# Shift and scale in couples, tokens in pairs of tiles, sums by transposes, Toeplitz products in column groups

## The chip, the cores and the metric

The kernel runs on one core of one Trainium2 chip. The metric is the device time of one execution in microseconds (us), as a median over runs.

## The reference, cut to what matters

One layer of a diffusion backbone: 1024 latent tokens and 256 context tokens of width 1024. The first two of six modulation vectors (a shift and a scale, from `c` for the latent tokens and from `c_ctx` for the context) act on the normalised tokens; one projection `w_in` follows. Its first 256 columns feed a bidirectional S5 (state space) block, the rest six gated heads over chunks of 128 tokens. After an output projection come a residual, a layer norm and a mixture of 16 experts.

```python
mod_lat = (silu(c) @ w_ada + b_ada)          # 6 vectors of 1024: sh1, sc1, g1, sh2, sc2, g2
mod_ctx = (silu(c_ctx) @ w_ada + b_ada)
z  = (layer_norm(x)   * (1 + sc1)  + sh1)  @ w_in
zc = (layer_norm(ctx) * (1 + csc1) + csh1) @ w_in[:, :256]
mix = concat(s5(z[:, :256], zc), heads(gelu(z[:, 256:]))) @ w_out
x_new = layer_norm(ALPHA * x + g1 * mix)
out = layer_norm(ALPHA * x_new + g2 * expert_choice_moe(modulate(x_new, sh2, sc2)))
```

In float32; large products are made as three products of a high and a low part (`wh`, `wl`, `xmH`, `xmL`).

## The kernel before

Every engine works its own queue in the order in which the program was written out; there is no scheduler. Ten token tiles of 128 rows are `items` 0 and 1 (context) and 2 to 9 (latent). For each, `tok_stats` and `tok_norm` normalise the rows on VectorE with two small GpSimd steps for the root, `tok_turn` transposes the tile on TensorE in two halves, `tok_mod` scales and shifts it on ScalarE (eight 128-wide activations and two copies that give `xmH`) and takes `xmL` on VectorE. Then `z_s5` projects the tile onto the S5 columns (24 products) and stores the result, and `unit` runs one head on one latent tile: 24 products in `head_a`, activation, statistics, and a small product in `head_p` three units later.

Shift and scale come from eight pieces of `w_ada` of 1 MB each, 256 outputs a piece. `ada_piece` multiplies one in four column groups of 32 (16 passes on TensorE, since a float32 product takes two); `ada_cols` then sums the four groups and turns the result into columns by a product with `combo`. All eight pieces are worked before anything is modulated; `mod1` is finished in two VectorE operations, and the loop over tiles starts. The S5 block runs as two generators, `lift_flow` and `s5_flow`; `pull` advances them between tile steps. Its set-up (`params`) works with many small operations on VectorE, and one part, `turns`, on GpSimd. `toeplitz` makes, four times, a small matrix from 8 products with 32 weights each, adds the diagonal and sends it through DRAM. `ada_b` turns later pieces into the second shift and scale. `conv_w` splits a weight block into `wh` (ScalarE) and `wl` (VectorE; for the S5 columns a quarter on GpSimd). Transposes write to two PSUM banks (`trp`), products to two (`mm`).

TensorE's queue does the pieces, waits for what it needs, and goes on to heads, output projection, router, and 528 blocks of expert weights. SyncE issues the loads in the order of `START`; a load waits for an earlier one or for its buffer.

Of the kernel before, what the change touches and what calls it, by code (L numbers as in the profile page):

```python
# [10 lines left out]
F32 = mybir.dt.float32  # L11
# [17 lines left out]
PULL0 = 9  # L29
# [21 lines left out]
MDVE = ()  # L51
START = "a0 a1 a2 a3 a4 a5 x0 a6 a7 w0 x1 x2 p w1".split()
PULLA = 2
# [9 lines left out]
PULLS = 2  # L63
W8 = 6
W9 = 8
N1 = 0
XB = 3
# [6 lines left out]
class S5:  # L74
# [7 lines left out]
    def __init__(self, nc, pool, psum, psum_tr, ident, id2, dcol):  # L82
        self.nc, self.ps, self.ptr = nc, psum, psum_tr
        self.ident, self.id2, self.dcol = ident, id2, dcol
        self.half = [pool, pool]
# [60 lines left out]

    def load_c(self, src):
        self.pc = self.t("pc", 2, 256).rearrange("p a b -> p (a b)")
        self.nc.sync.dma_start(self.pc, src[:, 560:1072])

    def params(self):
# [37 lines left out]
        self.turns(nc.gpsimd, cs, parts(1344, 4, 8), pw2, sq2, w[:, 22:24])  # L189
# [30 lines left out]
        yield  # L220

# [11 lines left out]

        t4, pw = parts(384, 4, 8), parts(896, 2, 10)
# [6 lines left out]
    def turns(self, v, cs, t, pw, sq, ph):  # L241
# [4 lines left out]
        self.cmul(b, a, a, t1, v)  # L246
        c = [x[:, :, 1:2] for x in pw]
        self.cmul(c, b, b, t1, v)
        self.cmul(b, c, c, t1, v)

# [7 lines left out]
        steps = self.powers(pw, b, 16, t, sq, v)  # L258
        while True:
            try:  # L260
                next(steps)
            except StopIteration as e:
                w8 = e.value
                break
# [64 lines left out]
    def toeplitz(self, q, dma, tz):  # L329
        nc, v = self.nc, self.nc.vector  # L330
        t0 = self.t("t0", 2, 16, 16)[0:32]
        ps = self.ptr()
        for d in range(2):
            for r in range(2):
                cc = d * 2 + r
                for i in range(2):
                    nc.tensor.matmul(ps[0:32, cc * 128:(cc + 1) * 128], self.bz[i][:, cc, :],
                                     self.cx[i][:, cc, d:d + 8, :].rearrange("p b h -> p (b h)"),
                                     start=(i == 0), stop=(i == 1))
        x = ps.rearrange("p (d r b h) -> p d r b h", d=2, r=2, b=8)[0:32]  # L340
        nc.scalar.activation(t0[:, :, 7:15, :], x[:, 0], AF.Copy)
        nc.scalar.activation(t0[:, :, 0:7, :], x[:, 1, :, 0:7], AF.Copy)
        nc.scalar.activation(t0[:, :, 15, :], x[:, 1, :, 7], AF.Copy)
        yield "pause"
        v.tensor_tensor(t0[:, :, 7], t0[:, :, 7], t0[:, :, 15], OP.add)
        for r in range(2):
            v.scalar_tensor_tensor(t0[:, r, 7, :], self.id2[0:32], self.dcol[0:32, 2 * q + r:2 * q + r + 1],
                                   t0[:, r, 7, :], op0=OP.mult, op1=OP.add)
        yield "pause"
        dma(tz[q], t0.rearrange("p r b h -> p (r b h)"))  # L350
# [83 lines left out]
def block_kernel(ctx: ExitStack, tc: tile.TileContext, a: dict, out: bass.AP):  # L434
# [35 lines left out]
    src = [a["w_ada"][i] for i in range(8)] + [a["w_in"][i] for i in range(3)]  # L470
# [119 lines left out]
    s5 = S5(nc, A_, acp2, trp, ident, off["id2"], off["dcol"])  # L590
    s5.load(a["s5par"])

# [26 lines left out]
    def tok_turn(i):  # L619

        if i >= NI:
            return
        xt = tok.pop(i)[0]
        turned[i] = []
        for half in range(2):
            p = trp()
            for c in range(4):
                k = 4 * half + c
                pe.transpose(p[:, c * 128:(c + 1) * 128], xt[:, k * 128:(k + 1) * 128], ident)
            turned[i].append(p)  # L630

    def take(i):

        kind, t = items[i]
        s = slice(t % 2 * 128, t % 2 * 128 + 128)
        return [x[:, :, s] for x in xm[kind, t // 2]]

    def tok_mod(i, parts=(0, 1)):

        if i >= NI:  # L640
            return
        kind, t = items[i]
        if t % 2 == 0 and 0 in parts:
            xm[kind, t // 2] = [slot(n, "big", [128, 8, 256], F32R) for n in ("xmH", "xmL")]
        mod = mod1[:, :, 0 if kind == "x" else 1]
        hi, lo = take(i)
        for half in parts:
            p = turned[i][half]
            t = X_.tile([128, 4, 128], F32, name="xmt", bufs=2)
            for c in range(4):  # L650
                k = 4 * half + c
                x = p[:, c * 128:(c + 1) * 128]
                if (i, half) in MDVE:
                    v.tensor_scalar(t[:, c], x, mod[:, 8 + k:9 + k], mod[:, k:k + 1], op0=OP.mult, op1=OP.add)
                else:
                    act.activation(t[:, c], x, AF.Identity, scale=mod[:, 8 + k:9 + k], bias=mod[:, k:k + 1])
            s = slice(4 * half, 4 * half + 4)
            act.activation(hi[:, s], t, AF.Copy)
            v.tensor_tensor(lo[:, s], t, hi[:, s].bitcast(F32), OP.subtract)

    def ada_piece(i, p):

        t = raw.pop(i).rearrange("p (k n) -> p k n", k=8)
        for r in range(2):
            for c in range(4):
                k = 2 * c + r
                pe.matmul(p[32 * c:32 * c + 32], s_t[:, k, :], t[:, k, :], start=(r == 0), stop=(r == 1),
                          tile_position=(0, 32 * c))

# [27 lines left out]
    def z_s5(i):  # L697
# [4 lines left out]
        p = mm()  # L702
        proj(p[:, 0:256], *take(i), ws5)
        z = X_.tile([128, 256], F32, name="zs5", bufs=2)
        act.activation(z, p[:, 0:256], AF.Copy)
# [152 lines left out]
    pull(PULL0)  # L858
    tok_stats(0)
    tok_norm(0)  # L860
    pull(PULLA)
    cols1 = acp2()
    ws = W_.tile([128, 6, 128], F32, name="ws")

    def ada_cols(i, rows):
        for c in range(2):
            k = 2 * i + c
            pe.matmul(cols1[:, 2 * k:2 * k + 2], rows[:, c * 128:(c + 1) * 128], combo[:, 0:2], start=True, stop=True)

    rows = []  # L870
    for i in range(8):
        p = mm()
        ada_piece(i, p[:, 0:256])
        rows.append(X_.tile([128, 256], F32, name="arow", tag="xmt", bufs=2))
        act.activation(rows[i], p[:, 0:256], AF.Copy)
        if i:
            ada_cols(i - 1, rows[i - 1])
    ada_cols(7, rows[7])
    tok_turn(0)
    c1 = cols1[:, 0:32].rearrange("p (c o) -> p c o", o=2)  # L880
    v.tensor_tensor(mod1, c1, bc(bcol[:, 0:16], [128, 16, 2]), OP.add)
    v.tensor_scalar(mod1[:, 8:16], mod1[:, 8:16], 1.0, None, op0=OP.add)
    tok_load(3)
# [87 lines left out]
    def ada_b(n):  # L971
# [8 lines left out]
        for c in range(4):  # L980
# [883 lines left out]
```

## Time and profile before

| | |
|---|---|
| median of 3 runs | 2026.65 us (2026.36 to 2029.82) |
| the profiled execution: time, span | 2030.29 us, 2028.5 us |
| mean granted TensorE clock | 0.994 |
| TensorE busy | 1971.9 us, 97% of the span |
| VectorE, ScalarE, GpSimd busy | 84%, 65%, 14% |
| bytes read from memory | 620.79 MB |

Times in the rows below are microseconds from the start of the span. A row in brackets names idle time of the engine just ahead of the instruction and what ended it. Matmul rows overlap, so the distance of two starts says more than a length.

### The profile page before, as it was taken

The numbers are of one execution on the slowest core, as the hardware profiler recorded it, in microseconds if no ns is written. First come the engines' busy times: TensorE is split into PE (matmuls) and PEld (weight loads), VectorE is DVE, ScalarE is ACT, GpSimd is POOL, SyncE is SP. The second block draws the span as 40 slices with busy tenths as digits, with TensorE's granted clock in tenths as the row PEclk, the third lists the DMA queues.
The fourth block names the chain that finished last, engine by engine and source line by source line (L and its number), as shares of the span: only waits on it lengthen the run. The fifth ranks groups of instructions, "written<-read, shape, count | busy, mean of one in ns | idle before, by whom it ended". The sixth has DMA issues, their size and how long they took to land. (4 is left out here: it accounts for less than half of the span.)

```text
span 2028.5 us, 27963 instructions
## 1 busy us (share of the span) xinstructions
PE 1971.9 (97%) x10690; PEld 1601.8 (79%) x10690; DVE 1709.7 (84%) x1770; ACT 1325.6 (65%) x1497; POOL 287.8 (14%) x462
## 2 busy tenths in 40 slices
PE   6999999989999999999999999999999999999997
PEld 4988897856788787888888888888788888888874
DVE  7678756978798988888898989898989888888876
ACT  3854453224677677767777777767777777677773
POOL 4343353120010101010000101010101010100024
PEclk9999999999999999999999999999999999999999
DMA  8244336379999999999999999999999999999795
GB/s 320 83 151 143 103 115 230 117 281 364 335 388 362 383 362 387 363 377 366 378 359 387 363 380 367 378 373 367 375 371 378 361 384 358 391 362 362 283 385 193
DMA packets 105434, 648.32 MB, mean 320 GB/s; under 512 B 11794, under 2 KB 19986, under 8 KB 33236
## 3 DMA queue, kind: packets, MB, share of 16 engines
q1 hardware_dynamic: 88788, 614.00, 79.0%
q0 software_dynamic: 6080, 23.87, 4.3%
q10 hardware_dynamic: 10432, 8.66, 1.3%
q8 instruction: 84, 1.38, 0.3%
q14 instruction: 50, 0.41, 0.1%
HBM read 620.79 MB, written 24.40 MB: 318 GB/s over the span
## 5 line engine op out<-in xcount | busy, mean ns | idle before, releaser
L1629 DVE TENSOR_TENSOR el<-raw,eh 128x2048 fp32r<-128x2048 f32 x513 | 1174.6, 2290 | 169.1 <-ACT eh L1628 147.7
L1628 ACT ACTIVATE eh<-raw 128x2048 fp32r<-128x2048 f32 x513 | 963.5, 1913 | 67.0 <-PE ac L1724 46.1
L1696 PE MATMUL mm<-eh,XH 128*128 128x512 f32 (+1 forms) x1484 | 566.3, 382 | 0.0
L1697 PE MATMUL mm<-el,XH 128*128 128x512 f32 (+1 forms) x1484 | 557.4, 376 | 0.0
L1698 PE MATMUL mm<-eh,XL 128*128 128x512 f32 (+1 forms) x1484 | 557.2, 375 | 0.0
L1697 PEld LDWEIGHTS mm<-el,XH 128*128 128x128 f32 x1484 | 279.6, 188 | 54.4 <-DVE el L1629 2.9
L1698 PEld LDWEIGHTS mm<-eh,XL 128*128 128x128 f32 x1484 | 279.6, 188 | 53.2
L1696 PEld LDWEIGHTS mm<-eh,XH 128*128 128x128 f32 x1484 | 279.5, 188 | 52.0 <-ACT raw L1562 1.2
L1722 PE MATMUL ac<-eh,tH 128*128 128x512 f32 x692 | 276.0, 399 | 0.0
L1724 PE MATMUL ac<-eh,tL 128*128 128x512 f32 x692 | 272.8, 394 | 0.0
L1723 PE MATMUL ac<-el,tH 128*128 128x512 f32 x692 | 272.2, 393 | 0.4 <-DVE el L1629 0.4
L1734 POOL DMA_INDIRECT acc_d<-yt,idx x15 | 50.7, 3381 | 1156.5 <-DVE yt L1732 1156.5
L1701 ACT ACTIVATE hs<-mm 128x512 f32<-128x512 f32 x96 | 54.1, 563 | 205.2 <-PE mm L1698 201.8
L1724 PEld LDWEIGHTS ac<-eh,tL 128*128 128x128 f32 x692 | 129.9, 188 | 30.3
L1723 PEld LDWEIGHTS ac<-el,tH 128*128 128x128 f32 x692 | 129.9, 188 | 29.7 <-DVE el L1629 0.8
L1722 PEld LDWEIGHTS ac<-eh,tH 128*128 128x128 f32 x692 | 130.0, 188 | 28.5 <-issue 0.5
L691 PE MATMUL mm<-wh,xmH 128*128 128x256 f32 x464 | 136.7, 295 | 5.7 <-ACT uv L905 5.7
L692 PE MATMUL mm<-wl,xmH 128*128 128x256 f32 x464 | 132.3, 285 | 2.5 <-DVE wl L686 2.5
L693 PE MATMUL mm<-wh,xmL 128*128 128x256 f32 x464 | 132.2, 285 | 0.0
L1648 ACT ACTIVATE tH<-tr 128x512 fp32r<-128x512 f32 x94 | 52.9, 562 | 92.7 <-PE tr L1640 91.7
L691 PEld LDWEIGHTS mm<-wh,xmH 128*128 128x128 f32 x464 | 89.8, 193 | 10.6 <-ACT uv L905 7.8
L1210 ACT ACTIVATE xgt<-tr,mod 128x128 f32<-128x128 f32 x124 | 55.5, 454 | 59.7 <-PE tr L1523 59.6
(416 smaller groups left out, 2092.4 us busy)
## 6 DMA issues: line engine op xcount, KB each, us to landing
raw<-in_w_moe SPq DMA_DIRECT2D x523, 1024.0 KB
raw<-in_w_ada SPq DMA_DIRECT2D x24, 1024.0 KB
raw<-in_w_in SPq DMA_DIRECT2D x7, 1024.0 KB
raw<-in_w_moe POOLq DMA_DIRECT2D x5, 1024.0 KB, 10.3
xt<-in_x SPq DMA_DIRECT2D x8, 512.0 KB
raw<-in_w_out SPq DMA_DIRECT2D x4, 1024.0 KB
xr<-in_x SPq DMA_DIRECT2D x8, 512.0 KB
acc_d<-accst ACTq DMA_DIRECT2D x8, 512.0 KB
```

The lines of the kernel that those rows point to most:

```text
L691: pe.matmul(p, xh[:, k], w[0][:, k], start=(k == 0), stop=False)
L692: pe.matmul(p, xh[:, k], w[1][:, k], start=False, stop=False)
L693: pe.matmul(p, xl[:, k], w[0][:, k], start=False, stop=(k == 7))
L1210: act.activation(out, p, AF.Identity, scale=mod2[:, 8 + k:9 + k], bias=mod2[:, k:k + 1])
L1628: act.activation(h, x, AF.Copy)
L1629: v.tensor_tensor(l, x, h.bitcast(F32), OP.subtract)
L1696: pe.matmul(p, XH[:, k], hh[:, c], start=(k == 0), stop=False)
L1697: pe.matmul(p, XH[:, k], ll[:, c], start=False, stop=False)
L1698: pe.matmul(p, XL[:, k], hh[:, c], start=False, stop=(k == 7))
L1722: pe.matmul(y, tH[:, sl], hh[:, c, m], start=first, stop=False)
L1723: pe.matmul(y, tH[:, sl], ll[:, c, m], start=False, stop=False)
L1724: pe.matmul(y, tL[:, sl], hh[:, c, m], start=False, stop=last)
```

## The change

The eight pieces are now worked in couples: a piece of the shift and the piece of the scale for the same 256 columns (0 and 4, 1 and 5, 2 and 6, 3 and 7). Each piece's row is copied to SBUF, turned by two transposes (`ada_turns`), and VectorE sums the four groups out of PSUM and adds the bias (`ada_mod`). After each couple a quarter of the channels can be modulated, and `z_part` adds this quarter to the S5 projection of both context tiles. Tokens go in pairs of tiles: `pair_turn` and `pair_mod` work a quarter of the channels of two tiles at a time, with scalings of 256 columns. `turns` becomes a generator that `side` advances between the other steps. The token loads are spread between the pieces. In the loop, pair g+1 is transposed and modulated while pair g is projected. `toeplitz` puts its products side by side in four column groups and adds the diagonal in one operation from a prepared tile; its result is stored by two transfers for one. `ada_b` sums by transposes too.

```diff
-START = "a0 a1 a2 a3 a4 a5 x0 a6 a7 w0 x1 x2 p w1".split()
+START = "x0 a0 a4 x1 a1 a5 w0 x2 a2 a6 x3 a3 a7".split()
-XB = 3
+XB = 4
...
-        self.turns(nc.gpsimd, cs, parts(1344, 4, 8), pw2, sq2, w[:, 22:24])
+        self.side = self.turns(nc.gpsimd, cs, parts(1344, 4, 8), pw2, sq2, w[:, 22:24])
...
     def toeplitz(self, q, dma, tz):
-        t0 = self.t("t0", 2, 16, 16)[0:32]
+        t0 = self.t("t0", 8, 16)
         ps = self.ptr()
-        for d in range(2):
+        for i in range(2):
+            for half in range(2):
+                for r in range(2):
+                    cc = (1 - half) * 2 + r
+                    o = 64 * half + 32 * r
+                    nc.tensor.matmul(ps[o:o + 32, 0:128], self.bz[i][:, cc, :],
+                                     self.cx[i][:, cc, 1:9, :].rearrange("p b h -> p (b h)"),
+                                     start=(i == 0), stop=(half == 1 and i == 1), tile_position=(0, o))
+        for i in range(2):
             for r in range(2):
-                cc = d * 2 + r
-                for i in range(2):
-                    nc.tensor.matmul(ps[0:32, cc * 128:(cc + 1) * 128], self.bz[i][:, cc, :],
-                                     self.cx[i][:, cc, d:d + 8, :].rearrange("p b h -> p (b h)"),
-                                     start=(i == 0), stop=(i == 1))
+                nc.tensor.matmul(ps[32 * r:32 * r + 32, 112:128], self.bz[i][:, r, :], self.cx[i][:, r, 0, :],
+                                 start=False, stop=(i == 1), tile_position=(0, 32 * r))
...
-    def tok_turn(i):
...
+    def pair_turn(g, j, p, tiles=(0, 1)):
+        for n in tiles:
+            for c in range(2):
+                k = 2 * j + c
+                pe.transpose(p[:, 256 * c + 128 * n:256 * c + 128 * n + 128],
+                             tok[2 * g + n][0][:, k * 128:(k + 1) * 128], ident)
+        turned[g, j] = p
...
-    def tok_mod(i, parts=(0, 1)):
...
+    def pair_mod(g, j):
...
+        for c in range(2):
+            k = 2 * j + c
+            act.activation(t[:, c], p[:, 256 * c:256 * c + 256], AF.Identity, scale=mod[:, 8 + k:9 + k],
+                           bias=mod[:, k:k + 1])
+        s = slice(2 * j, 2 * j + 2)
+        hi, lo = xm[g]
+        act.activation(hi[:, s], t, AF.Copy)
+        v.tensor_tensor(lo[:, s], t, hi[:, s].bitcast(F32), OP.subtract)
...
+    def ada_turns(j, s, rows):
+        if s == 0:
+            at_c[j] = acp()
+        for c in range(2):
+            o = 256 * s + 128 * c
+            pe.transpose(at_c[j][:, o:o + 128], rows[:, c * 128:(c + 1) * 128], ident)
+
+    def ada_mod(j):
+        c = W_.tile([128, 4, 2], F32, name="c1", bufs=2)
+        x = at_c[j].rearrange("p (m g r) -> p m r g", g=4, r=32)[:, :, 0:2]
+        v.tensor_reduce(c, x, axis=mybir.AxisListType.X, op=OP.add)
...
+    pair_mod(0, 1)
     ws5 = conv_w(8, W8)
...
+    rows = [ada_rows(4)]
+    tok_norm(2)
+    ada_turns(2, 0, rows[0])
+    z_part(0)
+    z_part(1)
+    rows.append(ada_rows(5))
+    ada_turns(2, 1, rows[1])
+    ada_mod(2)
+    pair_mod(0, 2)
+    tok_stats(3)
+    side(2)
+    pull(1)
+    tok_norm(3)
+    z_part(2)
...
-        for c in range(4):
-            pe.matmul(p[:, 2 * c:2 * c + 2], rows[:, c * 128:(c + 1) * 128], combo[:, 0:2], start=True, stop=True)
         j = 4 * (n - 2)
+        ada_turn(p, rows, m, 1)
...
-    for i in range(NI):
...
+    for g in range(1, NI // 2):
+        last = g == NI // 2 - 1
...
+        ahead = (0, 1, 2, 3) if g > 1 else (None, 0, 1, 2)
+        for j in range(4):
+            pairwise = g > 1 and not last
+            n = j // 2 if pairwise else j % 2
+            if not last and ahead[j] is not None:
+                pair_turn(g + 1, ahead[j], trp())
+            if j in ((0, 2) if pairwise else (0, 1)):
+                z_s5(2 * g + n)
+            else:
+                unit(2 * g - 2 + n)
+            if not last and ahead[j] is not None:
+                pair_mod(g + 1, ahead[j])
...
+            if j in (0, 2):
+                tok_stats(2 * g + 4 + j // 2)
+            else:
+                tok_norm(2 * g + 4 + j // 2)
+            pull(PULL1 if g > 1 or j == 3 else 0)
```

On ScalarE, in the ramp: `arow` is the copy of a piece's row out of PSUM, `xmt` a scaling, `xmH` the high part, `wh` the high part of the S5 weights. Before:

```order
L875 ACTIVATE arow<-mm 128x256 [waits PE_49] x2
L875 ACTIVATE arow<-mm 128x256 [waits PE_49,Activation_49] x6
L683 ACTIVATE wh<-raw 128x2048 [waits DMAHW5_49]
L656 ACTIVATE xmt<-tr,mod_125 128x128 [waits DVE_49,PE_49,Activation_49]
L656 ACTIVATE xmt<-tr,mod_125 128x128 x3
L658 ACTIVATE xmH<-xmt 128x4x128 [waits DMAHW4_49,Activation_49]
```

and in the change, from the fourth piece's copy on:

```order
L876 ACTIVATE arow<-mm 128x256 [waits PE_49]
L652 ACTIVATE xmt<-tr,mod_126 128x256 [waits DVE_49]
L652 ACTIVATE xmt<-tr,mod_126 128x256
L656 ACTIVATE xmH<-xmt 128x512 [waits Activation_49]
L689 ACTIVATE wh<-raw 128x2048 [waits DMAHW4_49]
L876 ACTIVATE arow<-mm 128x256 [waits PE_49] x2
```

All eight row copies stood ahead of the weights; now the weights stand between the fourth copy and the last four, behind two couples of scalings.

On TensorE, `tr<-sp,xt` are token transposes and the other rows products. Before, the transposes of item 5 behind the second head unit:

```order
L692 MATMUL mm<-wl,xmH 128x256
L693 MATMUL mm<-wh,xmL 128x256
L629 MATMUL tr<-sp,xt 128x128 [waits DVE_49,Activation_49]
L629 MATMUL tr<-sp,xt 128x128 x3
L629 MATMUL tr<-sp,xt 128x128 [waits Activation_49]
L629 MATMUL tr<-sp,xt 128x128 x3
L691 MATMUL mm<-wh,xmH 128x256 [waits Activation_49]
L692 MATMUL mm<-wl,xmH 128x256
```

and in the change, at the end of the loop's first trip, behind the second head unit:

```order
L698 MATMUL mm<-wl,xmH 128x256
L699 MATMUL mm<-wh,xmL 128x256
L634 MATMUL tr<-sp,xt 128x128 [waits PE_49,Activation_49]
L634 MATMUL tr<-sp,xt 128x128 x3
L634 MATMUL tr<-sp,xt 128x128 [waits DVE_49,PE_49,Activation_49]
L634 MATMUL tr<-sp,xt 128x128
L634 MATMUL tr<-sp,xt 128x128 [waits DVE_49]
L634 MATMUL tr<-sp,xt 128x128
```

Here the transposes of two pairs follow each other; the second group needs both tiles of the next pair normalised, its last two rows the second of them.

On VectorE at the same place, `xt<-xt,mv,rstd` is a normalisation and `xmL` the low part of a modulated tile. Before, the normalisation of item 4 with its statistics ahead:

```order
L582 BN_STATS st<-xt 128x6 [waits DMAHW5_49]
L582 BN_STATS st<-xt 128x6
L562 BN_AGGR mv<-st 128x2 [waits DVE_49]
L617 TENSOR_SCALAR xt<-xt,mv,rstd 128x1024 [waits DVE_49,PE_49,Pool_49]
L659 TENSOR_TENSOR xmL<-xmt,xmH 128x4x128 [waits Activation_49] x2
```

and in the change the second normalisation of that next pair:

```order
L657 TENSOR_TENSOR xmL<-xmt,xmH 128x512 [waits Activation_49]
L591 BN_STATS st<-xt 128x6 [waits DMAHW3_49]
L591 BN_STATS st<-xt 128x6
L571 BN_AGGR mv<-st 128x2 [waits DVE_49]
L657 TENSOR_TENSOR xmL<-xmt,xmH 128x512 [waits Activation_49]
L627 TENSOR_SCALAR xt<-xt,mv,rstd 128x1024 [waits DVE_49,PE_49,Pool_49]
```

The normalisation stood right behind its statistics and ahead of the subtractions of item 3; now a subtraction of the pair in work stands between a tile's statistics and its normalisation.

## Rows read from the trace of the kernel before

**Rows 1.** Windows view, stretches in us; busy time per engine (instructions), clock, DMA share, GB/s

```profile
10.00:20.00 10.00, 9.54 (x73) 4.41 (x74) 8.94 (x54) 1.47 (x5) 6.96 (x32) 1.00 1.01 423
...
315.00:320.00 5.00, 4.47 (x11) 3.27 (x12) 4.49 (x5) 3.04 (x8) 3.92 (x4) 0.66 0.42 150
...
600.00:1000.00 400.00, 399.35 (x1906) 326.70 (x1905) 355.98 (x224) 294.98 (x228) 23.73 (x8) 1.00 0.98 373
```

**Rows 2.** Timeline of TensorE, 9 to 65 us; start, length, line, operation, idle before

```profile
9.94 1.94 PE L667 MATMUL mm<-raw,s_t 128*32 128x256 f32 x16 [9.94 <-DMA raw<-in_w_ada]
...
39.95 1.94 PE L629 MATMUL tr<-sp,xt 128*128 128x128 f32 x8 [4.82 <-DVE xt L617]
...
41.90 0.41 PE L692 MATMUL mm<-wl,xmH 128*128 128x256 f32 x1
...
42.12 0.41 PE L693 MATMUL mm<-wh,xmL 128*128 128x256 f32 x1
...
50.25 0.36 PE L691 MATMUL mm<-wh,xmH 128*128 128x256 f32 x1
...
53.20 0.28 PE L691 MATMUL mm<-wh,xmH 128*128 128x256 f32 x1
...
54.57 0.39 PE L692 MATMUL mm<-wl,xmH 128*128 128x256 f32 x1 [1.09 <-DVE wl L686]
...
64.57 1.03 PE L629 MATMUL tr<-sp,xt 128*128 128x128 f32 x8
```

**Rows 3.** Timeline of ScalarE, 31 to 73 us

```profile
31.93 1.90 ACT L683 ACTIVATE wh<-raw 128x2048 fp32r<-128x2048 f32 x1
...
34.36 1.50 ACT L656 ACTIVATE xmt<-tr,mod 128x128 f32<-128x128 f32 x4 [0.53 <-PE tr L629]
...
36.43 1.49 ACT L656 ACTIVATE xmt<-tr,mod 128x128 f32<-128x128 f32 x4
...
71.39 0.28 ACT L904 ACTIVATE uv<-mm 128x128 f32<-128x128 f32 x1 [1.33 <-PE mm L693]
...
72.20 0.48 ACT L930 ACTIVATE uv<-uv,hst 128x128 f32<-128x128 f32 x1
```

**Rows 4.** Timeline of VectorE, 13 to 44 us

```profile
13.82 0.17 DVE L201 TENSOR_TENSOR scr<-scr,par 128x16 f32<-128x16 f32 x1
...
15.26 0.46 DVE L215 TENSOR_TENSOR bbr<-scr,par 128x256 f32<-128x256 f32 x1
...
17.98 0.11 DVE L223 TENSOR_TENSOR scr<-scr 128x16 f32<-128x16 f32 x1
...
35.28 1.71 DVE L686 TENSOR_TENSOR wl<-raw,wh 128x1536 fp32r<-128x1536 f32 x1
...
42.84 0.81 DVE L617 TENSOR_SCALAR xt<-xt,mv,rstd 128x1024 f32<-128x1024 f32 x1 [1.00 <-POOL rstd L564]
...
43.56 0.68 DVE L659 TENSOR_TENSOR xmL<-xmt,xmH 128x512 fp32r<-128x512 f32 x1
```

**Rows 5.** Timeline of GpSimd, 35 to 42 us

```profile
35.46 1.61 POOL L563 TENSOR_SCALAR rstd<-mv 128x1 f32<-128x1 f32 x1 [5.09 <-DVE mv L562]
...
41.93 0.22 POOL L563 TENSOR_SCALAR rstd<-mv 128x1 f32<-128x1 f32 x1 [2.68 <-DVE mv L562]
```

**Rows 6.** Timeline of TensorE, 109 to 316 us

```profile
109.16 0.39 PE L692 MATMUL mm<-wl,xmH 128*128 128x256 f32 x1 [1.38 <-DVE wl L686]
...
112.32 1.07 PE L667 MATMUL mm<-raw,s_t 128*32 128x256 f32 x16
...
119.79 0.41 PE L337 MATMUL tr<-cx,bzr 128*32 128x128 f32 x2 [0.25 <-ACT U L768]
...
121.66 0.38 PE L691 MATMUL mm<-wh,xmH 128*128 128x256 f32 x1
...
315.53 0.50 PE L1040 MATMUL mm<-woH,mh 128*128 128x512 f32 x1 [3.73 <-ACT mh L1026]
```

**Rows 7.** Waits of TensorE, 100 to 350 us: total, times, longest

```profile
PE mm L691 <- ACT uv L905: 5.7, 6, 1.7
```

More of the change, by code (lines that the diff above doesn't have):

```diff
@@ L28 @@
 PPE = 33
-PULL0 = 9
 PULL1 = 1
@@ L62 @@
 TLEAD = 2
-PULLS = 2
 W8 = 6
 W9 = 8
-N1 = 0
-XB = 3
+XB = 4
 def bc(ap, shape):
@@ L232, in params @@
         yield
+        for _ in self.side:
+            pass
         t4, pw = parts(384, 4, 8), parts(896, 2, 10)
@@ L257, in turns @@
             v.tensor_tensor(b[c], b[c], x, OP.mult)
[L258 to L264, printed above, removed]
+        yield
+        w8 = yield from self.powers(pw, b, 16, t, sq, v)
         self.cmul([x[:, :, 3:4] for x in sq], w8, w8, t1, v)
@@ L857, in block_kernel @@
     mod2 = K.tile([128, 16], F32, name="mod2")
[L858 to L862, printed above, removed]
-    ws = W_.tile([128, 6, 128], F32, name="ws")
[L865 to L871, printed above, removed]
+    bias1 = W_.tile([128, 2, 8], F32, name="bias1")
+    pool.tensor_copy(bias1, bcol[:, 0:16].rearrange("p (s k) o -> p s (k o)", s=2))
@@ new lines, in block_kernel, with z_part @@
+    zp = bank("rk")
+    zps = [zp[:, 256 * n:256 * n + 256] for n in range(2)]
+    def z_part(j):
+        for n in range(2):
+            proj(zps[n], *take(n), ws5, (2 * j, 2 * j + 1), n == 0, n == 1)
+    pull(2)
+    tok_stats(0)
+    pull(1)
+    tok_norm(0)
+    rows = [ada_rows(0)]
+    pull(1)
+    side(1)
+    rows.append(ada_rows(1))
+    ada_turns(0, 0, rows[0])
+    ps = [trp(), trp(), bank("sp"), bank("sp")]
+    for j in range(4):
+        pair_turn(0, j, ps[j], (0,))
+    ada_turns(0, 1, rows[1])
@@ new lines, in block_kernel @@
+    tok_load(4)
+    tok_stats(1)
+    ada_mod(0)
+    side(1)
+    pull(1)
+    tok_norm(1)
+    rows = [ada_rows(2)]
+    for j in range(4):
+        pair_turn(0, j, ps[j], (1,))
+    tok_load(5)
+    load_pre(9)
+    s5.load_c(a["s5par"])
+    ada_turns(1, 0, rows[0])
+    pair_mod(0, 0)
+    pull(1)
+    side(2)
+    rows.append(ada_rows(3))
+    ada_turns(1, 1, rows[1])
+    ada_mod(1)
+    pair_mod(0, 1)
+    ws5 = conv_w(8, W8)
+    tok_stats(2)
+    side(1)
+    rows = [ada_rows(4)]
+    tok_norm(2)
@@ new lines, in block_kernel @@
+    ada_turns(2, 0, rows[0])
[6 more added lines that the diff above has]
+    tok_stats(3)
+    side(2)
+    pull(1)
+    tok_norm(3)
+    z_part(2)
+    rows = [ada_rows(6)]
+    ada_turns(3, 0, rows[0])
+    for j in range(2):
+        pair_turn(1, j, trp())
+        pair_mod(1, j)
+    rows.append(ada_rows(7))
+    pair_turn(1, 2, trp())
+    ada_turns(3, 1, rows[1])
+    ada_mod(3)
+    tok_stats(4)
+    pair_mod(0, 3)
```

177 lines of the change are left out of this document (82 added, 95 removed).

## The prediction

> **What bounds the kernel now.** I read the windows first. From 600 to 1000 us TensorE is busy 399.35 of 400 us at clock 1.00 while the transfers run at a share of 0.98 [rows 1]: the expert stage is one dense stream of products, its loads are released by TensorE's progress, and the change does not touch it. Whatever the front of the kernel loses or wins therefore moves the whole stream, if nothing in between swallows it. So I read the front by TensorE's timeline. It starts at 9.94 us, when the first modulation piece lands, works through eight pieces and the first tile's transposes, and then stands 4.82 us, until 39.95, because the second tile is not yet normalised [rows 2]. Its products start cold: 0.22 us apart at 41.90 and 42.12; the 24 products from 50.25 to 53.20 stand 0.12 apart [rows 2]. At 50.25 the first latent tile's S5 projection starts, and by 65.4 (transposes at 64.57 plus 0.8) four S5 projections, two head units and the transposes of six tiles are done [rows 2]. I use that state as the milestone, because the changed order reaches the same state at the end of its first trip of the loop.
>
> **Loads.** Between 10 and 20 us 423 GB/s arrive [rows 1], so 2.48 us for a 1.05 MB piece. In the new order one token tile stands ahead of the first piece (11.2 instead of 9.94), and seven pieces, four tiles and one projection weight ahead of or at the eighth: 9.94 + (7 x 1.05 + 4 x 0.52 + 1.05)/0.423 = 34.7 us. With loads alone to wait for, the ramp would end soon after. I find it ends much later, because each piece now hangs in a chain through four engines that wait in program order.
>
> **The ramp, step by step.** Piece 2 of the load order lands at 13.7 and takes 1.9 [a piece: rows 2]. Tile 0's eight transposes (1.6), two turns of sums (0.5 each) and piece 3 follow, to 20.2. The transposes of tile 1 wait for VectorE: the sum's reduction and addition (about 0.5, two small operations), eight S5 operations (13.82 to 15.26, 1.44) and the normalisation (0.81) [rows 4] put them at 21.2. Transposes, a turn, a piece, its evacuation and turn: 26.6. On VectorE 2.7 us of S5 (15.26 to 17.98) [rows 4] stand ahead of the second reduction, so the couple is modulated from 27.5. A scaling couple on ScalarE: four 128-wide scalings and a copy repeat every 2.07 (34.36 to 36.43) [rows 3]; two 256-wide ones and the same copy I take at 1.65 (bounds 1.3 and 2.07). Then ScalarE's queue has the weight conversion of 1.90 [rows 3] ahead of the fifth piece's evacuation, and TensorE, whose next instruction needs that row, stands about 3 us. VectorE's share of the weights takes 1.71 [rows 4]: the first S5 product of the context pair runs at about 32.9.
>
> After that, each of the last two couples costs TensorE a hole: evacuation 0.6, (turn), reduction and addition 0.55, scalings 1.65, subtraction 0.68 [rows 4] = 3.3 to 3.5 us in which its queue offers nothing but the products that wait for them. To the first latent projection: 24 products (2.9 warm, 5.1 cold), piece 1.0 to 1.9 (16 passes take 1.07 warm [rows 6]), hole 3.8 with the turn, 12 products 1.4 to 2.6, piece and evacuation 1.9 to 2.8, a late normalisation up to 1.0, eight transposes 1.2 to 1.8, piece 1.0 to 1.9, transposes 0.6 to 0.9, two scaling couples ahead of the last evacuation 1.7, turn 0.3 to 0.5, hole 3.2, 12 products 1.4 to 2.6, transposes 0.6 to 1.0. The sum is 22 to 30, so 55 to 63 us against 50.25. I take 57.5: cold until the products are dense. From there to the milestone 96 products at 0.12 and 16 transposes plus 0.4 of waiting, 14.3 us: 71.8 against 65.4. **Term 1: +6.4 (3.9 to 11.9).**
>
> One rule bears on the 1.71: here VectorE and GpSimd begin their shares of the conversion together. In the trace a GpSimd operation that takes 0.22 took 1.61 beside that conversion [rows 5]. The Trainium skill, "SBUF — State Buffer", section "SBUF: two separate sides", says that the two engines share a port pair as an exclusive lock, held for a whole instruction, so that the loser blocks. By that rule VectorE would wait for GpSimd's whole share or not at all, and the trace's 1.61 agrees with blocking; the sum would grow by at most about the 1.4 that the blocked operation lost. I leave it at nothing.
>
> **The loop over pairs.** Now each trip starts with transposes that need the pair's second normalisation, and that stands on VectorE behind the last subtraction of the trip before, which stands behind ScalarE's work on the last unit. After unit 1: activation and square 0.81 (71.39 to 72.20) [rows 3], scalings 1.65, subtraction 0.68, normalisation 0.81 [rows 4] = 3.95, less the four transposes that TensorE still has. **Term 2: +3.5 (3.2 to 3.7).** After unit 3 ScalarE has one operation more (0.48) [rows 3]: 4.4 less 0.3. **Term 3: +4.1 (3.3 to 4.2).** In the last trip a projection needs the same trip's last couple for its fourth quarter: 3.6 less 18 products and a unit's small product, **term 4: +1.2 (0.5 to 1.5).** Before, transposes run a tile ahead and nothing of the kind shows.
>
> After a wait of 3.73 TensorE's clock fell: it was 0.66 between 315 and 320 us, between its two levels, 1.2 and 2.4 GHz [rows 1, 6], 0.34 x 5 = 1.7 us lost. Terms 2 and 3 are holes of that size. **Term 5: +1.7 (0 to 3.4).**
>
> **What it saves.** Toeplitz products: 16 passes from 119.79 to 121.66, 1.87 us [rows 6], four times. In four column groups 16 passes of twice the width took 1.07 [rows 6]; here 16 passes and 8 short ones, between 0.5 (half the width, short ones free) and 1.5 (no gain from width). I take 1.0: **term 6: -3.5 (-1.5 to -5.5).** The Trainium skill, "TensorEngine Tiling (Array Packing)", section "Theoretical Speedup", gives up to fourfold for 32 columns; by that 1.87 would become 0.47 and the term -5.6, which no row here reaches. The column sums of the second modulation: eight passes become four transposes; at about 0.1 us a transpose (eight end after 1.03 [rows 2]) and as much a pass, which loads the same 128x128 weights, 0.45 four times: **term 7: -1.8 (-1.8 to 0).** The 1.38 at 109.16 [rows 6], where unit 8 waits for weights, goes, since they are now converted two units earlier: **term 8: -1.4 (-1.4 to 0).** The smaller ScalarE work (1.65 for 2.07), GpSimd's spread S5 steps, one VectorE addition for three in Toeplitz and one more store issue there lie beside TensorE's products; uncovered, they would give or cost some 0.5 us per place.
>
> Sum: 6.4 + 3.5 + 4.1 + 1.2 + 1.7 - 3.5 - 1.8 - 1.4 = +10.2 us. The profiled execution has a span of 2028.5 and a time of 2030.29, 3.6 above the median of 2026.65; its span would be 2038.7, and the median 2026.65 + 10.2 = 2036.9. I say 2036.5. All terms at their low ends give about +2, all at their high ends +23.
>
> **Rivals.** (a) *The ramp keeps pace with the loads.* If a couple's chain fits into the 5.0 us between its two pieces, as the small transfers and the idle ScalarE (1.47 busy of 10 us [rows 1]) would allow, the eighth piece at 34.7, its 1.9, the hole of 3.8, 12 products and four transposes bring the latent projection to 43.5, 7 us sooner than now; with terms 2 to 8 (+3.8) that is -3, and without the clock's fall and with Toeplitz at its best -7: 2020 to 2024. It decides where that projection starts before about 46. Against it stand the conversion ahead of the fifth evacuation and the S5 work ahead of the second reduction, both in queues that cannot pass them. Chance 0.15.
> (b) *The lag is swallowed.* Head units wait for ScalarE's activation buffers 5.7 us in six places [rows 7]; if these waits follow the stores of the heads and not TensorE's pace, up to 5.7 goes and with the savings at their best the sum is within 4: about 2029. For it: the six waits are real; against: they follow the spacing of units, which a late start does not change. Chance 0.20.
> (c) *The clock stays low in the ramp and falls after every hole*: term 1 at 11.9, term 5 at 3.4, sum +17: 2044. Before, the pieces and transposes never brought the spacing to 0.12 by 42 us, which speaks for it; dense products from the context pair on speak against. Chance 0.20. The forecast holds 0.45.
>
> **Range and chances.** The measurement tells about 0.2%, 4 us, from no change. (a) gives faster 0.15, (b) same 0.20, the forecast (2031 to 2041) and (c) slower 0.65. A range from 2025 to 2045 leaves out most of (a) and the extremes of (c).
>
> **What would show it.** Right: TensorE stands about 3 us ahead of the fifth sum's turn, released by ScalarE; twice 2.5 to 3.5 us ahead of context products, released by ScalarE or VectorE; the first latent S5 projection starts at 55 to 63; two waits of 3 to 4.5 us at token transposes, released by VectorE's normalisation, each followed by low clock; Toeplitz blocks near 1 us; the expert stage keeps its 399.35 us for 1906 TensorE instructions [rows 1]. Wrong: the projection starts before 50, or those two waits are under 1 us, or the lag at the milestone is gone by 330 us.

## The result and the profile after

The changed kernel takes 2042.64 us (median of 4, 2041.23 to 2042.92) where the kernel before takes 2027.57 (2026.36 to 2029.82, one run more than in the table above): ratio 1.0074, 95% interval 1.0061 to 1.0087, so 15.1 us slower. The profiled execution has a span of 2041.1 us and a mean granted clock of 0.984 (0.994 before). Direction and order of size are as forecast; terms 2, 3 and 5 of the sum are not.

The windows, with the columns of [rows 1]. The second group is one row of the kernel before and one of the kernel after, for the stretch from the milestone to the first piece of the second modulation:

```profile
10.00:20.00 10.00, 8.42 (x61) 4.34 (x61) 8.39 (x36) 1.58 (x5) 5.63 (x22) 1.00 1.01 423
...
600.00:1000.00 400.00, 399.34 (x1914) 326.77 (x1913) 356.87 (x229) 294.43 (x228) 26.36 (x9) 1.00 0.98 375
```

```profile
65.40:112.32 46.92, 44.56 (x374) 43.45 (x372) 24.81 (x61) 35.89 (x106) 18.36 (x46) 1.00 0.21 59
```

```profile
72.10:136.54 64.44, 49.79 (x374) 48.04 (x373) 34.52 (x128) 32.05 (x86) 23.03 (x54) 0.87 0.17 54
```

The expert stage is the same stream as in [rows 1]; the loss is ahead of it. The last two rows hold the same 374 products and transposes: TensorE stands 14.65 us among them for 2.36 (64.44 less 49.79; 46.92 less 44.56), and is busy 5.2 us longer, at a clock of 0.87 for 1.00. That is 17.5 us in one stretch, where I had forecast 9.1 (terms 2 to 5, less term 8).

TensorE's timeline of the changed kernel:

```profile
10.22 1.93 PE L665 MATMUL mm<-raw,s_t 128*32 128x256 f32 x16 [10.22 <-DMA raw<-in_w_ada]
...
19.96 0.66 PE L634 MATMUL tr<-sp,xt 128*128 128x128 f32 x4 [0.88 <-DVE xt L627]
...
29.47 0.69 PE L885 MATMUL ac<-sp,arow 128*128 128x128 f32 x2 [2.73 <-ACT arow L876]
29.81 0.56 PE L697 MATMUL rk<-wh,xmH 128*128 128x256 f32 x1
...
40.31 0.58 PE L697 MATMUL rk<-wh,xmH 128*128 128x256 f32 x1 [2.20 <-ACT xmH L656]
...
53.96 0.58 PE L697 MATMUL rk<-wh,xmH 128*128 128x256 f32 x1 [2.45 <-ACT xmH L656]
...
57.70 0.56 PE L697 MATMUL mm<-wh,xmH 128*128 128x256 f32 x1
...
71.51 0.60 PE L634 MATMUL tr<-sp,xt 128*128 128x128 f32 x4
78.04 0.69 PE L634 MATMUL tr<-sp,xt 128*128 128x128 f32 x2 [5.94 <-ACT xmt L652]
80.16 0.69 PE L634 MATMUL tr<-sp,xt 128*128 128x128 f32 x2 [1.42 <-DVE xt L627]
...
100.80 0.69 PE L634 MATMUL tr<-sp,xt 128*128 128x128 f32 x2 [5.42 <-DVE xt L627]
...
114.75 1.12 PE L634 MATMUL tr<-sp,xt 128*128 128x128 f32 x4 [1.03 <-ACT xmt L652]
```

The first latent projection starts at 57.70 (50.25 in [rows 2]), the milestone is reached at 71.51 + 0.6 = 72.1 (65.4). Then the first transposes of each trip of the loop wait: 5.94 and 1.42 us, 5.42 us, and 1.03 us. The lag behind the kernel before, by the same instruction in both:

| | before | after | lag |
|---|---|---|---|
| first latent S5 projection | 50.25 | 57.70 | 7.5 |
| milestone | 65.4 | 72.1 | 6.7 |
| first piece of the second modulation | 112.32 | 136.54 | 24.2 |
| first Toeplitz block | 119.79 | 144.00 | 24.2 |
| first product of the output projection | 315.53 | 330.57 | 15.0 |
| first expert product | 461.7 | 476.8 | 15.1 |

**The first wait.** ScalarE, GpSimd, VectorE and SyncE ahead of 78.04, from their timelines, and SyncE's waits from 20 to 110 us (in all, times, longest):

```profile
76.59 0.40 ACT L1001 ACTIVATE hjunk<-uv,hst 128x128 bf16<-128x128 f32 x1 [4.35 <-POOL hst L992]
...
76.99 1.00 ACT L652 ACTIVATE xmt<-tr,mod 128x256 f32<-128x256 f32 x2
...
73.81 0.55 POOL L572 TENSOR_SCALAR rstd<-mv 128x1 f32<-128x1 f32 x1 [8.45 <-DVE mv L571]
...
76.00 0.55 POOL L992 TENSOR_SCALAR hst<-hst 128x1 f32<-128x1 f32 x1
...
72.19 1.29 DVE L591 BATCH_NORM_STATS2 st<-xt 128x6 f32<-128x512 f32 x2 [7.75 <-DMA xt<-in_x]
...
64.47 0.33 SPq L531 DMA_DIRECT2D raw<-in_w_ada  x1
64.89 7.83 SPq L617 DMA_DIRECT2D xt<-in_x  x4
```

```profile
SPq L531 <- DVE wl L692: 27.5, 2, 24.5
```

Read it from the bottom. SyncE stands up to 24.5 us at a weight load, whose buffer is free only when the second weight's conversion has ended; the loads of tiles 6 and 7 stand behind it in the same queue and go out from 64.89 on (the row's x4 holds tiles 8 and 9 too). Tile 6 lands at 72.19, VectorE has waited 7.75 us for it, GpSimd's root waits for VectorE, the head unit's small step (`hst`) stands behind that root on GpSimd, ScalarE waits 4.35 us for that step with the scalings behind it, and TensorE waits for a transpose bank that the scalings free. One late load goes through four queues.

**The second wait.** VectorE ahead of 100.80:

```profile
97.78 0.20 DVE L116 COPY scr<-scr 128x16 f32<-128x16 f32 x1 [1.91 <-POOL scr L109]
...
99.34 0.68 DVE L657 TENSOR_TENSOR xmL<-xmt,xmH 128x512 fp32r<-128x512 f32 x1
99.94 0.81 DVE L627 TENSOR_SCALAR xt<-xt,mv,rstd 128x1024 f32<-128x1024 f32 x1
```

ScalarE's `xmH` of that quarter is done at 97.85, but the subtraction starts at 99.34: VectorE first waits 1.91 us for GpSimd's part of the S5 set-up and works 14 small operations of its own part.

**The clock behind the waits**, in windows of 2 us:

```profile
80.00:82.00 2.00, 1.84 (x9) 1.85 (x10) 2.00 (x14) 0.22 (x1) 1.00 (x3) 0.50 0.03 8
82.00:84.00 2.00, 2.00 (x12) 2.00 (x12) 0.12 (x1) 0.00 (x0) 0.00 (x0) 0.58 0.00 0
84.00:86.00 2.00, 2.00 (x19) 2.00 (x18) 0.00 (x0) 0.94 (x3) 0.25 (x1) 1.00 0.00 0
...
102.00:104.00 2.00, 2.00 (x11) 2.00 (x11) 0.17 (x2) 0.00 (x0) 0.00 (x0) 0.50 0.00 0
...
116.00:118.00 2.00, 2.00 (x12) 2.00 (x11) 0.08 (x1) 0.79 (x2) 0.00 (x0) 0.54 0.00 0
```

Nine to twelve products fit into 2 us at 0.50 to 0.58, at or near the lower of the two levels, and 19 at 1.00; behind the third wait (1.03 us at 114.75) the clock falls too.

**What is saved.** A Toeplitz block and one turn of sums, TensorE's timeline:

```profile
144.00 0.42 PE L345 MATMUL tr<-cx,bzr 128*32 128x128 f32 x8 [0.25 <-ACT U L775]
144.25 0.40 PE L345 MATMUL tr<-cx,bzi 128*32 128x128 f32 x8
144.46 0.22 PE L350 MATMUL tr<-cx,bzr 128*32 128x16 f32 x4
144.52 0.22 PE L350 MATMUL tr<-cx,bzi 128*32 128x16 f32 x4
144.67 0.39 PE L697 MATMUL mm<-wh,xmH 128*128 128x256 f32 x1
...
229.82 0.60 PE L672 MATMUL mm<-sp,arow 128*128 128x128 f32 x4
```

and a turn of sums in the kernel before:

```profile
211.36 0.95 PE L981 MATMUL mm<-sp,arow 128*128 128x2 f32 x8
```

0.67 us a block where [rows 6] has 1.87, and 0.60 for four transposes where the eight passes took 0.95.

### The profile page after: what moved, and what is told of

It reads as the page before. It is cut to its first block, busy times and chain, and to the rows that moved or that the text cites. A ratio compares the mean times of both kernels' runs of the same rounds, so it can differ in the third digit from the quotient of the medians.

```text
span 2041.1 us, 27908 instructions
## 1 busy us (share of the span) xinstructions
PE 1967.9 (96%) x10690; PEld 1598.2 (78%) x10690; DVE 1706.9 (84%) x1772; ACT 1315.4 (64%) x1449; POOL 291.0 (14%) x466
## 3 DMA queue, kind: packets, MB, share of 16 engines
q8 instruction: 84, 1.38, 0.3%
```

## The experiments

Each kernel was timed against runs of the kernel before on the same chip; the ratio is to those. There were four groups: e1 to e4 (kernel before at 2028.18), e5, e6 and the two b runs (2029.64), e7 to e9 (2027.66), and e10 (2029.17). Between groups the ratios are the safer comparison.

| run | edit, in words | median, us | ratio to before (95%) |
|---|---|---|---|
| e1_loads | tiles 6 and 7 loaded ahead of weights | 2044.38 | 1.0078 (1.0064 to 1.0092) |
| e2_mod | modulation right behind its transposes | 2037.28 | 1.0044 (1.0031 to 1.0058) |
| e3_loads_mod | both | 2034.95 | 1.0027 (1.0015 to 1.0040) |
| e4_loads_mod_norm | both, normalisation earlier | 2029.89 | 1.0007 (0.9997 to 1.0018) |
| e5_weights_last | e4, two weight loads later | 2027.30 | 0.9991 (0.9981 to 1.0002) |
| e6_warm | e5, long fillers in the ramp | 2024.24 | 0.9980 (0.9971 to 0.9989) |
| e7_warm_half | e5, short fillers | 2024.04 | 0.9978 (0.9968 to 0.9987) |
| e8_conv | e5, weight conversion earlier | 2021.23 | 0.9967 (0.9958 to 0.9976) |
| e9_conv_warm | e8 with short fillers | 2022.83 | 0.9970 (0.9959 to 0.9981) |
| e10_buffer | e9, a seventh activation buffer | 2008.30 | 0.9898 (0.9881 to 0.9914) |
| b_toep | before, Toeplitz in column groups | 2023.25 | 0.9972 (0.9962 to 0.9982) |
| b_toep_adab | the same, sums by transposes | 2022.87 | 0.9976 (0.9966 to 0.9985) |

### The two waits of the loop: four kernels

**e1_loads**

```diff
+    for i in (6, 7):
+        tok_load(i)
     wc = conv_w(9, W9)
     nc.sync.dma_start(ws, a["gm_ws"])
     load_next()
     load_next()
...
-        if not last:
+        if not last and g > 1:
             tok_load(2 * g + 4)
```

> The loads of token tiles 6 and 7 stand ahead of the two weight loads in SyncE's queue. Queue theory (the wait of 5.94 and 1.42 us at the transposes of tiles 6 and 7 comes from a tile that lands at 72.2 us, because its load is issued behind a weight load that waits until 64.5 for the second weight's conversion): the tile lands near 62 us, and what is left of the wait is the 3.5 us of my forecast, ScalarE's work after unit 1; gain about 4 us, 2038.5. Rival (the load only happens to be the last of several late things, and ScalarE or GpSimd would keep TensorE waiting as long): the wait stays above 6 us, gain under 1.5 us, 2041 to 2043.

No gain at all, and yet the wait for the late load is gone. TensorE's and ScalarE's timelines of this kernel:

```profile
67.11 0.38 PE L697 MATMUL mm<-wh,xmH 128*128 128x256 f32 x1 [4.30 <-ACT zs L712]
...
76.96 0.44 PE L634 MATMUL tr<-sp,xt 128*128 128x128 f32 x2 [1.48 <-ACT xmt L652]
79.08 0.69 PE L634 MATMUL tr<-sp,xt 128*128 128x128 f32 x2 [1.68 <-DVE xt L627]
...
66.67 0.81 ACT L712 ACTIVATE zs<-mm 128x256 f32<-128x256 f32 x2 [7.34 <-DMA zk<-zs]
```

At the transposes 3.16 us are left, which is the forecast's own chain (3.5). In its place TensorE waits 4.30 us at a projection: ScalarE cannot empty the product bank, because `zs` has two buffers and both are held by stores (128 KB transfers into `zk`, another SBUF tile) that land after up to 9.0 us (median 3.0). The moved loads set those stores beside 3.5 MB of loads. Both theories of this run missed that: one wait was exchanged for another of the same size.

**e2_mod**

```diff
                 pair_turn(g + 1, ahead[j], trp())
+                pair_mod(g + 1, ahead[j])
             if j in ((0, 2) if pairwise else (0, 1)):
                 z_s5(2 * g + n)
             else:
                 unit(2 * g - 2 + n)
-            if not last and ahead[j] is not None:
-                pair_mod(g + 1, ahead[j])
```

> In the loop over pairs the modulation of a quarter stands right behind its transposes, ahead of the projection or unit, instead of behind it. Forecast's theory (the wait at the next trip's first transposes hangs on ScalarE's scalings behind the last unit's work): the second wait, 5.42 us at 95 to 101 us, falls to 2 to 3 us, the first one stays with the late load; gain 2.5 to 4.5 us with the clock, 2038 to 2040. Rival (VectorE's S5 steps and GpSimd set the second wait, not ScalarE's order): the second wait stays above 4.5 us, gain under 1.5 us.

2037.28, a little better than the 2038 to 2040 expected. The second wait is 3.05 us for 5.42, the 1.03 at the third trip is gone, and the first stays (3.84 and 3.67), as it must with the late load:

```profile
76.27 0.41 PE L634 MATMUL tr<-sp,xt 128*128 128x128 f32 x2 [3.84 <-DVE xt L627]
80.35 0.69 PE L634 MATMUL tr<-sp,xt 128*128 128x128 f32 x2 [3.67 <-DVE xt L627]
98.83 0.69 PE L634 MATMUL tr<-sp,xt 128*128 128x128 f32 x2 [3.05 <-DVE xt L627]
```

So the place of the modulation behind the unit, the mechanism of my terms 2 and 3, is real. What is left of the second wait stands in VectorE's own queue, where the subtraction and the normalisation (to 98.8) follow a wait for GpSimd and 14 small S5 operations:

```profile
95.80 0.20 DVE L116 COPY scr<-scr 128x16 f32<-128x16 f32 x1 [1.92 <-POOL scr L109]
```

**e3_loads_mod** has both edits.

> Both edits. If the two waits are separate, with a fall of the clock behind each: the first wait falls to under 1.5 us, the second to 2 to 3, gain 9 to 12 us, 2031 to 2034. Rival (swallowed: the front's lag is given back later in any case by the waits of the head units, so that a gain here is lost there): gain under 5 us, 2038 or more.

2034.95, a little above the expected range; the eleven times spread from 2029.0 to 2040.2, and the profile is of the longest. In it no wait is left at the transposes of tiles 6 and 7, 3.06 us at those of 8 and 9, but 4.64 at the projection behind the stores. The rival (2038 or more) does not fit.

**e4_loads_mod_norm**

```diff
-            if j in (0, 2):
-                tok_stats(2 * g + 4 + j // 2)
-            else:
-                tok_norm(2 * g + 4 + j // 2)
+            if j in (1, 2):
+                tok_norm(2 * g + 3 + j)
+            if j in (0, 1):
+                tok_stats(2 * g + 4 + j)
```

> Both edits, and the statistics and normalisation of a pair's second tile half a trip earlier, ahead of the S5 steps of that trip's end. Queue theory: no wait over 1 us is left at the transposes of the loop, the clock stays at its upper level from 62 us to the last trip, the lag at the first second-modulation piece falls from 24.2 to about 8 to 10 us; gain 13 to 17 us, 2025.5 to 2029.5, about the kernel before, with the ramp's 6.7 us set off by the smaller Toeplitz blocks and sums. Rival (swallowed): gain under 8 us.

2029.89, level with the kernel before. No transposes of the loop wait. The first piece of the second modulation runs at 120.1 for 136.5; 5.42 us at 67.07 are left, behind the same stores, with a clock of 0.83 from 60 to 80 us.

### The stores, and the ramp

**e5_weights_last**

```diff
     nc.sync.dma_start(ws, a["gm_ws"])
-    load_next()
-    load_next()
...
         if g == 2:
+            load_next()
+            load_next()
             ctx_done.append(1)
```

> As the kernel before it in the row (tile loads first, modulation behind its transposes, normalisation early), and the two weight loads of 1.05 MB issued only behind the loads of tiles 8 and 9. Theory (the wait of 5.42 us at 67 us comes from two stores of S5 projections that land 9.6 us after their issue, because 3.5 MB of loads are in flight beside them): the stores land within 4 us, that wait is under 1 us, no low clock behind it; gain 5 to 8 us on 2029.9, so 2022 to 2025, faster than the kernel before the change. Rival (the stores are slow by themselves or wait in GpSimd's queue): wait above 4 us, 2028 to 2031.

The wait falls from 5.42 to 0.69 us and the clock is 1.00 from 60 to 140 us. ScalarE finds the buffer free at 63.84, in e4 at 66.63, which is 2.8 us of the fall; the other 1.9 come from a ramp that is later in this profile (TensorE reaches the wait at 63.6 for 61.7). The time, 2027.30 where 2022 to 2025 was expected, is level with the kernel before. The gain in the profile's front is 4.8 us at the first later piece (115.3); the medians show 2.6 (3.2 by the ratios).

The stores did not come under 4 us (7.7 at most, 9.6 before), so that part of the expectation missed; 1.4 MB of loads still run beside them. Still, the landing goes with the loads in flight. From the issue of the first pair of stores to the free buffer it is 3.8 us in the changed kernel with no load beside them (60.35 to 64.15), 5.5 in e5 with 1.4 MB (58.38 to 63.84), and 9.1 in e1 and 9.7 in e4 with 3.5 MB (57.56 to 66.67, 56.98 to 66.63). ScalarE's rows of the changed kernel and of e5:

```profile
64.15 0.39 ACT L712 ACTIVATE zs<-mm 128x256 f32<-128x256 f32 x1 [2.04 <-DMA zk<-zs]
```

```profile
63.84 0.39 ACT L712 ACTIVATE zs<-mm 128x256 f32<-128x256 f32 x1 [3.70 <-DMA zk<-zs]
```

**e6_warm and e7_warm_half** fill TensorE's ramp waits with products that nobody reads:

```diff
+    def warm(n):
+        p = mm()
+        for _ in range(n):
+            pe.matmul(p[:, 0:128], ident, ident, start=True, stop=True)
...
+    warm(14)
     rows = [ada_rows(4)]
+    warm(20)
```

> The same, and in the ramp 14, 20, 18 and 20 products of the identity matrix with itself, whose result nobody reads, ahead of the fifth piece, behind it, and ahead of the third and fourth context products, in stretches where TensorE stood 2.0, 2.7, 2.2 and 2.5 us. Theory (the clock, 0.50 to 0.67 between 26 and 59 us, is a good part of the ramp's loss): the context products stand 0.12 apart instead of 0.21, the first latent S5 projection starts 4 to 6 us sooner, gain 3 to 6 us. Rival (the ramp is held by ScalarE's and VectorE's chains, and TensorE's pace only fills the time between): the products are closer together, but the projection starts under 2 us sooner, gain under 2 us.

> As the run with products of the identity matrix in the ramp, but 7, 9, 8 and 9 of them instead of 14, 20, 18 and 20, since each took two passes of 0.115 us and the four groups took 2.73, 4.73, 4.18 and 4.63 us where 2.0 to 2.7 us were free. Clock theory (the ramp's loss is in good part TensorE's low clock): the products between 30 and 56 us stand 0.12 apart, the groups end before what TensorE waits for, and the first latent S5 projection, at 55.3 with the long groups and 55.7 without any, starts at 51 to 53; 2 to 3 us less than with the long groups, 2021 to 2022.5. Rival (the chain of ScalarE, VectorE and loads holds the ramp): projection at 54 or later, 2023.5 to 2027.

In e6 the clock is 1.00 from 30 to 60 us, but the groups ran past their waits, and the projection starts at 55.26 against 55.73 in e5, as the rival had it. The median is lower than e5's all the same (3.1 us, 2.2 by the ratios); the profiled executions differ by 0.4, so this trace does not explain it. With the short groups the projection starts at 52.33:

```profile
35.89 1.95 PE L910 MATMUL mm<-sp 128*128 128x128 f32 x16
38.37 0.39 PE L697 MATMUL rk<-wh,xmH 128*128 128x256 f32 x1 [0.53 <-ACT xmH L656]
```

So the low clock costs the ramp about 3.4 us in e5's profile; the rest of its length is the chain, here with ScalarE still last. The time did not follow (2024.04 for 2024.24, where 2021 to 2022.5 was expected), which asked for the last experiment, e10.

**e8_conv and e9_conv_warm** put the first S5 weight's conversion ahead of the second quarter's scalings; e9 adds 7, 3, 8 and 9 fillers.

```diff
     ada_mod(1)
+    ws5 = conv_w(8, W8)
     pair_mod(0, 1)
-    ws5 = conv_w(8, W8)
```

> Without products of the identity matrix; the first S5 weight's conversion one place earlier, ahead of the scalings of the second quarter, where ScalarE stood 2.9 us for the second modulation couple. Forecast's theory (TensorE stands about 3 us ahead of the fifth sum's turn because the conversion of 1.89 us stands ahead of that piece's evacuation on ScalarE): that wait, 3.16 us, falls to 1 to 1.5 us, the first context product runs 1.5 to 2 us sooner, gain 1 to 2 us on 2027.3 if the ramp's later steps follow. Rival (loads or the last couples set the ramp's end, so the early gain is lost at the sixth piece): first context product sooner, projection within 0.7 us of 55.7, gain under 0.7 us.

> The earlier conversion and 7, 3, 8 and 9 products of the identity matrix. If both causes are real and stand in one chain, the first latent S5 projection starts at 49.5 to 51.5, earlier than or level with the kernel before the change (50.25), and the time is 2019 to 2021.5, below the kernel before with the column groups alone (2023.25). Rival (only one of the two is on the path): no better than the better of the two single edits.

In e8 the wait ahead of the fifth turn falls from 3.16 to 0.49 us, the first context product runs at 28.92 for 29.88, and the projection starts at 53.22. The median gains 6 us (4.9 by the ratios), more than the 2.5 at the projection explain; the profiled executions differ by 3.6. In e9 it starts at 49.41, ahead of the 50.25 of [rows 2], so the ramp can be made as short as before. The time (2022.83) is no better than e8's: the expectation's second half missed.

### Where the front's gain went

From e5 to e9 the first piece of the second modulation moves from 115.3 to 108.6, the output projection only from 313.0 to 310.1. Between them ScalarE's waits of e9, from 100 to 330 us:

```profile
ACT uv L999 <- DMA mix_d<-uv: 41.0, 16, 5.7
```

It waits for stores of head results to free one of six `uv` buffers, and TensorE waits 9.2 us behind it (the group of [rows 7]). The kernel's code says why one buffer can count: a unit's result is stored behind the activation of the fifth unit after it, and the sixth unit after it needs the buffer, so the store has one unit's time to land. **e10_buffer** has one buffer more (the row copies of the ramp share these buffers and have the same number):

```diff
-        uv = W_.tile([128, 256], F32, name="uv", bufs=LAG[3] + 2)
+        uv = W_.tile([128, 256], F32, name="uv", bufs=LAG[3] + 3)
```

> The kernel with the earlier conversion and the products of the identity matrix, and seven buffers instead of six for a head unit's activations. The front of that kernel reached the first second-modulation piece 6.7 us sooner than the kernel with the weights last (108.6 for 115.3), but the first output projection only 2.9 us sooner (310.1 for 313.0), while ScalarE waited 41.0 us in 16 places for stores of head results that hold a buffer, and TensorE 9.2 us in six places behind it. Swallowing theory (an earlier front runs into those stores, so that half of its gain is lost there): with one more buffer TensorE's six waits fall to under 4 us, the output projection starts at 304 to 307, gain 3 to 6 us on 2022.8, so 2017 to 2020. Rival (the waits follow the units' own chain through GpSimd and VectorE or the loads, and a buffer only moves them): waits above 7 us, gain under 1.5 us.

2008.30: 14.5 us less than e9 (14.6 by the ratios), and 1.0% (0.86 to 1.19) below the kernel before. The same stretch of both, from the first piece to the output projection, e9 first:

```profile
108.60:310.10 201.50, 184.71 (x1768) 166.42 (x1767) 140.88 (x297) 96.19 (x343) 90.14 (x207) 0.99 0.42 136
```

```profile
109.30:295.80 186.50, 182.57 (x1767) 164.91 (x1766) 141.16 (x296) 96.60 (x343) 92.77 (x207) 1.00 0.45 148
```

TensorE's idle time falls from 16.8 to 3.9 us, of which 3.6 stand ahead of the output projection; no wait is put down to a store any more, and 2.1 us of low clock go with the waits. ScalarE still stands 40.4 us ahead of the same operation in places for which the profile names no releaser, but TensorE does not wait behind them. I had expected 3 to 6 us, since I counted on a part of the 9.2 alone. In fact all of it goes, and with it 2.3 us of waits at the heads' small products and 1.5 of the 1.7 at the first Toeplitz block, which hung on the same ScalarE queue.

ScalarE waits for the same stores in the kernel before too, and there TensorE stands 5.7 us behind it [rows 7]:

```profile
ACT uv L904 <- DMA mix_d<-uv: 31.3, 12, 4.0
```

### The kernel before with single parts

**b_toep** takes the Toeplitz products, and **b_toep_adab** the transposed sums too, into the kernel before, with the code of the change.

> The kernel before with the Toeplitz blocks in column groups alone. Theory (TensorE is the bound there): the four blocks fall from 1.87 to the 0.67 us that the changed kernel shows, gain 3 to 5 us, 2023.5 to 2025. Rival (the head units' waits for ScalarE and the expert stage's start swallow it): gain under 2 us.

> The kernel before with the column groups and with the second modulation's sums by transposes. Forecast's term for the sums: 1.8 us more than with the column groups alone, 2021.5 to 2023.5. Rival (the reduction on VectorE or the head units' waits take it up): no more than 0.5 us more.

The column groups alone gain 5.7 us (3.7 to 7.7); of that 4 x 1.2 = 4.8 are the blocks. The sums add nothing that can be told (2022.87 for 2023.25), and the two intervals are too wide to tell the forecast's 1.8 us from nothing.

## Why the prediction was right or wrong

**Loads and ramp, term 1: right, in part by luck.** +6.4 forecast, +6.7 measured; projection at 57.5 forecast, 57.70 measured. The wait ahead of the fifth turn (2.73 for about 3) and the two ahead of context products (2.20 and 2.45 for 3.3 to 3.5) stand where I put them, released by ScalarE, the last two shorter than forecast. Inside, two errors cancel: the first context product is 3.1 us sooner than I said (29.81 for 32.9), and the clock is lower for longer (0.67, 0.52 and 0.66 in the three tens from 30 to 60 us). e7 shows the clock's part, e8 that of the conversion. The steps that I listed behind the first context product also add up to 21.0 to 30.8 us and not to 22 to 30, so the range for the projection should have read 54 to 64.

**VectorE's 1.71 beside GpSimd: right, left at nothing.** VectorE's share took 1.76, starting 0.04 us ahead of GpSimd's, which took 2.85. In the kernel before the same GpSimd share took 1.26; there it began 0.06 us ahead of a normalisation on VectorE, and the normalisation took 1.75 where another took 0.81 [rows 4]:

```profile
29.18 1.76 DVE L692 TENSOR_TENSOR wl<-raw,wh 128x1536 fp32r<-128x1536 f32 x1 [1.11 <-ACT wh L689]
29.22 2.85 POOL L692 TENSOR_TENSOR wl<-raw,wh 128x512 fp32r<-128x512 f32 x1 [7.53 <-ACT wh L689]
```

```profile
37.99 1.26 POOL L686 TENSOR_TENSOR wl<-raw,wh 128x512 fp32r<-128x512 f32 x1
38.05 1.75 DVE L617 TENSOR_SCALAR xt<-xt,mv,rstd 128x1024 f32<-128x1024 f32 x1 [0.46 <-POOL rstd L564]
```

The Trainium skill, "SBUF — State Buffer", section "SBUF: two separate sides", gives the port pair that the two share to the one that starts first and has the other block for the whole instruction; both pairs of rows agree.

**Term 2, +3.5: the step that failed.** 7.36 measured. I let the chain begin with ScalarE after unit 1 and took tile 7's load for granted. I had counted what the new order does to four engines, but not that it sets two weight loads ahead of two token loads in SyncE's queue. e1 removes the late load and leaves 3.16, so the chain that I described is there and rightly sized; in the changed kernel it was covered by a longer one, which starts at the landing of the late tile (72.19).

**Term 3, +4.1: 5.42.** Mechanism right (e2: 3.05 once the modulation stands earlier), size short by VectorE's wait for GpSimd and its S5 operations, which I had written off as lying beside TensorE's products: they put the subtraction off by 1.49 us (97.85 to 99.34), and without them the wait would be 3.9.

**Term 4, +1.2:** 1.03 at the third trip's transposes and 0.23 at the projection; the sum is right, but the place is a transpose bank and not the projection's fourth quarter.

**Term 5, +1.7: 5.2 measured**, above my bound of 3.4. The clock falls behind three waits instead of two, and stays down for 2 to 3 us of products each time (to 83.8, 104.2 and 117.9).

**Terms 6 to 8.** Toeplitz -4.8 for -3.5, inside its bounds. A block is 1.87/0.67 = 2.8 times as fast; its 16 wide products alone, 0.46 us (144.00 to 144.46), are 4.1 times as fast, and the 8 short ones, which I had put at nothing or little, take the other 0.21. The fourfold of the Trainium skill, "TensorEngine Tiling (Array Packing)", section "Theoretical Speedup", agrees with the wide ones; I had said that no row reaches it. Sums: 4 x 0.35 = -1.4 on TensorE for -1.8, nothing that can be told in the time. The 1.38 us wait for unit 8's weights is gone, as forecast.

**The sum.** Measured 6.7 + 17.5, and then 9.2 back by the output projection: TensorE is busy 7.9 us less from the first later piece to there (183.4 for 191.3: Toeplitz, sums, and a clock of 0.91 from 180 to 200 us that only the kernel before has) and idle 1.3 less. So 15.0, for 10.2. Rival (a) is out: even in e9, with two repairs, the projection starts at 49.41 and not at the 43.5 that it needs. Rival (b)'s mechanism is real but was worth little here: of the lag, 1.3 us were swallowed in TensorE's waits. Rival (c) named the number that came (2044), and its clock came too, low in the ramp and down behind every wait; but term 1 was not at its upper end, and the late load is not in it.

## What to carry to other kernels

When work is moved, write out the loads' queue as well as the engines': a load that waits for its buffer holds every load behind it, and the delay comes out four engines later under another name. When a front is made faster and the time does not follow, look for the next buffer that is held by a store; one more of them was worth more here (14.5 us) than any other single edit. That buffer was not tried in the kernel before, so how much of it belongs to the changed front stays open; the waits for the same stores that it has (31.3 us on ScalarE, 5.7 on TensorE behind them) speak for a part that does not.

## What the runs showed of the hardware

Small transfers landed late beside large loads: a 128 KB transfer of an S5 projection lands 3.0 us after its issue as a rule, but at most 7.7 us after it in e5 with 1.4 MB of loads under way, and 9.0 and 9.6 in e1 and e4 with 3.5 MB. Where VectorE and GpSimd began within 0.06 us of each other, the later one took longer: a weight conversion on GpSimd 2.85 us behind VectorE's share and 1.26 ahead of a normalisation, the normalisation 1.75 behind it and 0.81 elsewhere.
